# Attention's first two value projections: chunks taken in turn, and four sums in two wide PSUM tiles

## The chip, the cores and the metric

The kernel runs on one core of one Trainium2 chip. The metric is device time in microseconds (us) of one execution; lower is better. Times are medians of several runs. The profile is one execution more, taken by the hardware profiler; its span goes from the first to the last instruction.

## What is computed

The program is a decoder trunk of two layers on 256 tokens of width 1024 in float32. Each layer is a token mixer (stick-breaking attention beside MoBA attention, two branch projections, two sigmoid gates, one output projection) and a SwiGLU block, each followed by a residual and a layer norm. What matters here is the start of the mixer of the first layer:

```python
proj = x @ w_in
q_sb, k_sb, v_sb, q_mb, k_mb, v_mb, g_sb, g_mb = jnp.split(proj, cuts, axis=-1)
o_sb = stick_breaking_attention(heads(q_sb, 8), heads(k_sb, 8), heads(v_sb, 8))
o_mb = moba_attention(partial_rope(heads(q_mb, 8), pos), partial_rope(heads(k_mb, 8), pos), heads(v_mb, 8))
```

The first two outputs that the kernel makes are v_sb and v_mb, each 256 tokens by 512 columns.

## The kernel before, in words

**Products.** A float32 product is made of three passes of the rounded type float32r: both operands are split into a high part (a cast, `hi`) and a low part (the operand less its high part, `lo`), and TensorE adds hi·hi, hi·lo and lo·hi into one sum (`mm3`, whose matmuls all stand on L529). The cast runs on ScalarE (all on line L60, the helper `act`), the subtraction on VectorE (all on L65, the helper `dve`).

**Weights.** They come in chunks ("granules") of 128 x 1024 float32, 512 KB each, called by SyncE's queue into one of six `raw` buffers, and their two parts go into two rings `whi` and `wlo` of ten chunks each. A few chunks are split by DMA instead. The stream of chunks runs ahead of TensorE. A chunk's number is its place in the stream; the buffers are named after it, so `raw13` is chunk 13. The first four are loaded and split in two halves.

**What sets the order.** Each engine runs its instructions in the order in which they are written. The class `Weave` keeps an estimated clock while the program is written and decides by it where a chunk's split, or an eviction of a sum, is put among the instructions of ScalarE and VectorE. The very first splits stand in a table, `START`, with a time each.

**The start.** Twenty passes of zeros (`busy`, ten float32 matmuls of two recorded passes each) run on TensorE while the first data are on their way. `both_tokens` then makes v_sb (sums `l0pv0` and `l0pv1`, one for each half of the tokens, chunks 0 to 3) and after it v_mb (`l0pu0`, `l0pu1`, chunks 4 to 7). Chunk 0 is not split: `whole` multiplies it as float32 with the unsplit x (L564). The sums of v_sb lie in two PSUM tiles of one bank (the pool of `bankM`), those of v_mb in the first bank of two tiles of two banks (`banksB`). When a sum is done, `put` evicts it in two steps, a cast on ScalarE and a subtraction on VectorE, into `l0vsb` or `l0vmb`. Behind these stand the queries and keys (`l0pq`, `l0pk`, ...). Where an instruction writes a tile that another engine has read, the framework makes it wait on that engine's semaphore.

x itself comes transposed, in three pieces for each half of the tokens (`x00`, `x01`, `x02` for the first, `x10`, `x11`, `x12` for the second); ScalarE's queue loads the first four pieces, SyncE's the last two between the first chunks.

Of the kernel before, what the change touches and what calls it, by code (L numbers as in the profile page):

```python
# [10 lines left out]
AF = mybir.ActivationFunctionType  # L11
# [4 lines left out]
P = 128  # L16
# [5 lines left out]
WIDTH = 512  # L22
# [13 lines left out]
          ([("n", d)] if isinstance(d, int) else [("b", d[1]), ("a", d[0]), ("t", d[0]), ("u", d[0])])]  # L36
         for down in DOWN]
BASE = [sum(NG_LAYER - NFC + len(x) for x in STEPS[:l]) for l in range(DEPTH + 1)]
EARLY = [*range(4), *range(16, 20), 8, 14, 9, 15, *range(4, 8), 20, 24, 21, 25, *range(10, 14), 22, 23,
         *range(26, 40)]  # L40
NACT = 12
# [5 lines left out]
class Weave:  # L47
# [6 lines left out]
    def __init__(self):  # L54
        self.t = self.act_t = self.dve_t = self.pool_t = 0.0
        self.sides = []
        self.busy = False
# [51 lines left out]
class WeightStream:  # L109
# [2 lines left out]

    def __init__(self, nc, pool, w, total, weave, rings):
        self.nc, self.pool, self.w, self.total, self.weave = nc, pool, w, total, weave
        self.loaded, self.split = 0, NWHOLE
        self.done = -1
        self.free = {-1: 0.0}
        self.current = 0
        self.rings = rings
        self._lay()  # L120
        self.dma_t = 1.7
        self.raws, self.left = [], {0: 9.0}
        self.raw, self.parts, self.there, self.ready, self.dma = {}, {}, {}, {}, {}
# [61 lines left out]
    def put_aside(self, l, places):  # L185

        for g, parts in zip(filter(self.aside, range(BASE[l], BASE[l + 1])), places):
            self.parts[g] = parts
# [72 lines left out]
    def piece(self, g, i, e):  # L261

        if i == 0:
            self.parts[g] = tuple(ring[:, self.place[g]:self.place[g] + GCOLS] for ring in self.rings)
        (hi, lo), t, sl = self.parts[g], self.raw[g], self._pieces(g)[i]
        n = sl.stop - sl.start
        e = self.weave.act(e, n, self.nc.scalar.copy, hi[:, sl], t[:, sl])
        self.ready[g] = self.weave.dve(e, n, self.nc.vector.tensor_sub, lo[:, sl], t[:, sl], hi[:, sl].bitcast(F32))
        if sl.stop == GCOLS:
            self.raw.pop(g)  # L270
            self.left[g] = self.ready[g]
            self.split += 1
            self.load(g + 1 + NRAW)

# [6 lines left out]
    def take(self, g):  # L281
# [3 lines left out]
        while g in self.dma and g not in self.ready:  # L285
# [6 lines left out]
RING = 10 * GCOLS + LINES  # L292
NRAW = 6
NWHOLE = 1
START = (("x00", 4.4), ("x10", 5.4), ("x01", 6.4), ("w10", 6.4), ("w11", 7.4), ("x11", 7.4), ("w20", 8.2), ("x02", 9.0),
         ("w21", 9.7), ("x12", 10.3), ("w30", 11.0), ("w31", 11.7))
BY_DMA = ((18, 24, 28, 33, 38), (18, 24, 28, 33, 38))
ASIDE = ((), ())
X_AFTER = {(2, 0): (0, 2), (2, 1): (1, 2)}
NSPLIT = 10  # L300
HOLD = (8, 5)
FINE = 4
N_WARM = 10
LEAD = 2
LOAD = 1.46
DMA_HI = 6.0
# [12 lines left out]
def place(g):  # L319

    l, r = where(g)
    if r >= NG_LAYER - NFC:
        r = NG_LAYER - NFC + STEPS[l][r - (NG_LAYER - NFC)][1]
    return l * NG_LAYER + (EARLY[r] if r < len(EARLY) else r)


def where(g):

    l = sum(g >= b for b in BASE[1:-1])
    return l, g - BASE[l]  # L330

# [30 lines left out]
def hybrid_trunk_kernel(ctx: ExitStack, tc: tile.TileContext, w, xT_in, x_in, ln_in,  # L362
                        ident_in, mask_in, rope_in, out):
    nc = tc.nc
# [27 lines left out]
    def bankM(name, shape):  # L392
        ps = psM.tile(shape, F32, tag="M", name=name)
        m_last.append(bank_of(ps))
        if len(m_last) > 2:
            m_before[m_last[-1]] = m_last[-3]
            begin(ps)
        return ps
# [3 lines left out]
    def begin(ps):  # L402
        pe_after(m_free.get(m_before.get(bank_of(ps)), 0.0))

    def bank_of(ps):
        return getattr(ps, "tensor", ps).name
# [7 lines left out]
    def bankC(name, shape):  # L414
        held.append(weave.t)
        return psC.tile(shape, F32, tag="C", name=name)
# [31 lines left out]
    def banksB(name):  # L448
        return psB.tile([P, 2, 512], F32, tag="B", name=name)
# [12 lines left out]
    zero, mhalf = few[:, 0:1], few[:, 1:2]  # L462
# [6 lines left out]
    weave = Weave()  # L469
    ws = WeightStream(nc, wpool, w, BASE[-1], weave, (whi, wlo))  # L470
    act, dve, pool = weave.act, weave.dve, weave.pool
# [7 lines left out]
    warm = small.tile([P, 1], F32, tag="nmu", name="warm")  # L479
# [5 lines left out]
    busy = bankC("busy", [P, P])  # L485
    for i in range(N_WARM):
        nc.tensor.matmul(busy, zero.to_broadcast([P, P]), zero.to_broadcast([P, P]), start=True, stop=True)

    def load_xT(t, ks, queue):
        queue.dma_start(xT_raw[t][:, ks, :], xT_in[:, t, ks, :])  # L490
# [6 lines left out]

    kcs = [slice(0, 2), slice(2, 4), slice(4, 8)]
    ws.side = weave.add(ws.line(), last=True)
    for t, k in ((0, 0), (1, 0), (0, 1), (1, 1)):  # L500
        load_xT(t, kcs[k], nc.scalar)
    nc.scalar.activation(warm, zero, AF.Sigmoid)

    def between(g, i):
        if (g, i) in X_AFTER:
            t, k = X_AFTER[g, i]
            load_xT(t, kcs[k], nc.sync)

    ws.load(4, between)
    for (kind, a, b), e in START:  # L510
        if kind == "x":
            split_xT(int(a), kcs[int(b)], e)
        else:
            ws.piece(int(a), int(b), e)
    weave.t = 4.5

    def late_loads():
        nc.sync.dma_start(ident, ident_in)
# [16 lines left out]
    def mm3(o, s_hi, s_lo, m_hi, m_lo, start, stop, tick=True):  # L535
        mm(o, s_hi, m_hi, start, False)
        mm(o, s_hi, m_lo, False, False)
        mm(o, s_lo, m_hi, False, stop)
        if tick:
            weave.tick()  # L540
# [5 lines left out]
    def pe_after(e):  # L546
        weave.t = max(weave.t, e)
# [12 lines left out]
    def whole(o, g, t, first):  # L560

        raw = ws.raw[g].rearrange("p (k c) -> p k c", k=2)
        for k in range(2):
            nc.tensor.matmul(o, xT_raw[t][:, 2 * g + k, :], raw[:, k, :], start=first and k == 0, stop=False)  # L564
            weave.t += 4 * WIDTH / 2400.0
            weave.tick()

    def tok_major(o, g, t, first, last, k0):

        if g < NWHOLE:  # L570
            return whole(o, g, t, first)
        hi, lo = ws.take(g)
        hi = hi.rearrange("p (k c) -> p k c", k=2)
        lo = lo.rearrange("p (k c) -> p k c", k=2)
        for k in range(2):
            ts = slice(t * P, (t + 1) * P)
            mm3(o, xT_hi[:, k0 + k, ts], xT_lo[:, k0 + k, ts], hi[:, k, :], lo[:, k, :],
                first and k == 0, last and k == 1)

    def both_tokens(name, g0, put):  # L580

        acc = [banksB(f"{name}{t}")[:, 0, :] if g0 == 4 else bankM(f"{name}{t}", [P, WIDTH]) for t in range(2)]
        order = ((0, 0), (1, 0), (0, 1), (1, 1), (0, 2), (1, 2), (0, 3)) if g0 <= 4 else \
            ((0, 0), (0, 1), (0, 2), (1, 0), (1, 1), (0, 3), (1, 2))
        for t, k in order + ((1, 3),):
            tok_major(acc[t], g0 + k, t, k == 0, k == 3, 2 * k)
            if t == 1:
                ws.used(g0 + k)
            if k == 3:
                put(t, acc[t])  # L590

    def feat_major(o, g):

# [346 lines left out]
    for l in range(DEPTH):  # L940
        G = BASE[l]
        L = f"l{l}"
# [8 lines left out]
            split_v(v_mb[t], ps)  # L951

        if l == 0:
            both_tokens(f"{L}pv", G, put_v)
            both_tokens(f"{L}pu", G + 4, put_u)
        else:
            for t in range(2):
                weave.finish(norms[:t + 1])
                pe_after(xT_ready[t])
                for j, put in enumerate((put_v, put_u)):  # L960
                    ps = bankM(f"{L}pvu{j}{t}", [P, WIDTH])
                    for i in range(4):
                        g = G + 4 * j + i
                        tok_major(ps, g, t, i == 0, i == 3, 2 * i)
                        if t == 1:
                            ws.used(g)
                    put(t, ps)
# [64 lines left out]
        for d in range(2):  # L1032
            q, k = [qk["q", d][:, n] for n in range(2)], qk["k", d]
# [69 lines left out]
        for t in range(2):  # L1103
            acc = banksB(f"{L}pw{t}")
# [78 lines left out]
        for t in range(2):  # L1183
            weave.finish(norms[:t + 1])
            pe_after(xT_ready[t])
            for j in range(2):
                ps = bankM(f"{L}pft{t}{j}", [P, 512])
                for i in range(4):
                    g = G + 56 + 4 * j + i
                    tok_major(ps, g, t, i == 0, i == 3, 2 * i)  # L1190
                    if t == 1:
                        ws.used(g)
                sides.append(weave.start(h_line(f"{L}sg{t}{j}", ps, j, t)))
# [11 lines left out]
        acc = [banksB(f"{L}pd{t}") for t in range(2)]  # L1205
# [71 lines left out]
        g = G + NG_LAYER - NFC  # L1277
        late_half = []
        for n, d in enumerate(DOWN[l][:-HOLD[l]]):
# [16 lines left out]
            i = pairs.index(d)  # L1296
# [109 lines left out]
```

## Time and profile before

| | |
|---|---|
| median of 3 runs | 716.48 us (716.02 to 716.57) |
| the profiled execution | 716.68 us, its span 714.9 us |
| TensorE (PE) busy in the span | 706.7 us (99%) |
| weight loads (PEld), VectorE, ScalarE, GpSimd busy | 657.7, 599.5, 436.6, 35.0 us |
| HBM read | 139.69 MB, 197 GB/s over the span |
| first product of v_sb starts | 5.05 us |
| first product of the queries starts | 27.97 us |

PE is the matmul engine, PEld its weight loads, DVE VectorE, ACT ScalarE, SP SyncE, POOL GpSimd. A busy time is that of instructions on the engine; TensorE's matmuls overlap, so that its speed is read from the distance of their starts. In a timeline row stand the start, how long the row lasts (one instruction or several alike), the engine, the line, the operation, the tiles written and read, the count, and in brackets the idle time before it with what ended it. The rows of the changed kernel have the same names, with line numbers four or five higher.

### The profile page before, as it was taken

How to read it: one execution, taken by the hardware profiler on the slowest of the kernel's cores; microseconds unless marked ns; L12 is line 12 of the kernel's file. 1: busy time of each engine (PE TensorE's matmuls, PEld its weight loads, DVE VectorE, ACT ScalarE, POOL GpSimd, SP SyncE). 2: the span in 40 equal slices, each digit the busy share in tenths (PEclk: the TensorE clock that was granted, in tenths of full speed). 3: DMA queues.
4: the chain of work that ended last, by engine and by line, in shares of the span. 5: the costliest groups of instructions: out<-in, count | busy, mean ns of one | idle time of the engine just before them, and what ended most of it. 6: DMA issues, size and time to landing. Idle time of an engine off the chain costs nothing. (4 is left out here: it accounts for less than half of the span.)

```text
span 714.9 us, 13082 instructions
## 1 busy us (share of the span) xinstructions
PE 706.7 (99%) x5135; PEld 657.7 (92%) x5135; DVE 599.5 (84%) x920; ACT 436.6 (61%) x677; POOL 35.0 (5%) x61
## 2 busy tenths in 40 slices
PE   9999999999999999999999999999999999999995
PEld 7999999998899999988889999999888999999885
DVE  5989989797888777799887899987879878778987
ACT  5868977664565554456456787876456555544551
POOL 0200100000000000000000010000010000000002
PEclk9999999999999999999999999999999999999998
DMA  8977755565585664449559566745646856524451
GB/s 319 396 230 254 198 153 173 167 217 186 171 301 197 194 194 145 122 142 329 198 183 315 155 186 170 213 142 177 237 147 216 273 189 198 191 96 137 147 206 59
DMA packets 40526, 141.58 MB, mean 198 GB/s; under 512 B 4625, under 2 KB 5393, under 8 KB 40465
## 3 DMA queue, kind: packets, MB, share of 16 engines
q1 hardware_dynamic: 37008, 129.74, 53.1%
q0 software_dynamic: 2880, 10.49, 6.9%
q8 instruction: 40, 0.66, 0.4%
q10 hardware_dynamic: 576, 0.52, 0.2%
q14 instruction: 22, 0.17, 0.1%
HBM read 139.69 MB, written 1.05 MB: 197 GB/s over the span
## 5 line engine op out<-in xcount | busy, mean ns | idle before, releaser
L65 DVE TENSOR_TENSOR wlo<-raw,whi 128x1024 fp32r<-128x1024 f32 (+1 forms) x274 | 302.2, 1125 | 27.2 <-ACT whi L60 23.8
L60 ACT CAST whi<-raw 128x1024 fp32r<-128x1024 f32 (+1 forms) x274 | 260.2, 973 | 75.1 <-DVE raw L65 29.5
L529 PE MATMUL l0pf<-xT_hi,whi 128*128 128x256 f32 x288 | 79.6, 276 | 0.0
L529 PE MATMUL l1pf<-xT_hi,whi 128*128 128x256 f32 x288 | 79.6, 276 | 0.0
L529 PE MATMUL l0pf<-xT_lo,whi 128*128 128x256 f32 x288 | 79.5, 276 | 0.0
L529 PE MATMUL l0pf<-xT_hi,wlo 128*128 128x256 f32 x288 | 79.5, 276 | 0.0
L529 PE MATMUL l1pf<-xT_hi,wlo 128*128 128x256 f32 x288 | 79.5, 276 | 0.0
L529 PE MATMUL l1pf<-xT_lo,whi 128*128 128x256 f32 x288 | 79.5, 276 | 0.0
L529 PEld LDWEIGHTS l0pf<-xT_lo,whi 128*128 128x128 f32 x288 | 54.1, 188 | 0.0
L529 PEld LDWEIGHTS l1pf<-xT_lo,whi 128*128 128x128 f32 x288 | 54.1, 188 | 0.0
L529 PEld LDWEIGHTS l1pf<-xT_hi,whi 128*128 128x128 f32 x288 | 54.1, 188 | 0.0
L529 PEld LDWEIGHTS l0pf<-xT_hi,whi 128*128 128x128 f32 x288 | 54.1, 188 | 0.0
L529 PEld LDWEIGHTS l0pf<-xT_hi,wlo 128*128 128x128 f32 x288 | 54.1, 188 | 0.0
L529 PEld LDWEIGHTS l1pf<-xT_hi,wlo 128*128 128x128 f32 x288 | 54.1, 188 | 0.0
L529 PE MATMUL l0pg<-xT_hi,whi 128*128 128x256 f32 x128 | 35.8, 280 | 0.0
L529 PE MATMUL l1pg<-xT_hi,whi 128*128 128x256 f32 x128 | 35.8, 280 | 0.0
L529 PE MATMUL l0pg<-xT_hi,wlo 128*128 128x256 f32 x128 | 35.5, 277 | 0.0
L529 PE MATMUL l1pg<-xT_hi,wlo 128*128 128x256 f32 x128 | 35.5, 277 | 0.0
L529 PE MATMUL l1pg<-xT_lo,whi 128*128 128x256 f32 x128 | 35.5, 277 | 0.0
L529 PE MATMUL l0pg<-xT_lo,whi 128*128 128x256 f32 x128 | 35.5, 277 | 0.0
L65 DVE TENSOR_TENSOR l1sf<-l1sf,l1pf 128x256 f32<-128x256 f32 x36 | 15.1, 421 | 15.5 <-ACT l1sf L60 14.9
L60 ACT ACTIVATE l0sf<-l0pf 128x256 f32<-128x256 f32 x18 | 6.9, 385 | 31.2 <-PE l0pf L529 31.2
(485 smaller groups left out, 1941.0 us busy)
## 6 DMA issues: line engine op xcount, KB each, us to landing
raw<-in_w_dram SPq DMA_DIRECT2D x230, 512.0 KB, 4.2
whi<-in_w_dram POOLq DMA_DIRECT2D x10, 512.0 KB, 5.1
wlo<-in_w_dram POOLq DMA_DIRECT2D x10, 512.0 KB, 6.3
ln<-in_ln_dram SPq DMA_DIRECT2D x8, 512.0 KB, 5.9
raw<-in_w_dram SPq DMA_DIRECT2D x8, 256.0 KB, 4.6
x<-in_x_dram SPq DMA_DIRECT2D x2, 512.0 KB, 4.7
xT_raw<-in_xT_dram ACTq DMA_DIRECT2D x4, 128.0 KB, 4.8
xT_raw<-in_xT_dram SPq DMA_DIRECT2D x2, 256.0 KB, 5.1
```

Source lines behind the costliest of these rows:

```text
L60: f(*args, **kw)
L65: f(*args, **kw)
L529: nc.tensor.matmul(o, a, b, start=start, stop=stop)
```

## The change

1. **Chunks in turn.** The new list `FIRST` loads the chunks of v_sb and v_mb alternately (columns of `w_in` for v_sb on even places of the stream, for v_mb on odd ones), and `both_tokens` goes through both outputs together: for each of four steps, v_sb for both halves of the tokens, then v_mb for both.
2. **Four sums in two tiles.** There are now two tiles of two banks, one for each half of the tokens, named `l0pv0` and `l0pv1`. The first bank holds the sum of v_sb, the second that of v_mb. The tiles named `l0pu` are gone.
3. **Unsplit products for one half.** Chunk 0 is multiplied unsplit for the first half of the tokens only; for the second half it is split like all others, so that `START` has two entries more (`w00`, `w01`).
4. **Fourteen warming passes** (`N_WARM` 7) in place of twenty.
5. **Order of the first loads and splits.** ScalarE issues one load of x, then loads its activation table and runs its warming instruction, then issues the other three. `X_AFTER` puts the last two pieces of x one chunk later in SyncE's queue. `START` has other times and another order.

```diff
+FIRST = [0, 16, 1, 17, 2, 18, 3, 19]
...
-        self.loaded, self.split = 0, NWHOLE
+        self.loaded, self.split = 0, 0
...
         if sl.stop == GCOLS:
-            self.raw.pop(g)
-            self.left[g] = self.ready[g]
+            if g >= NWHOLE:
+                self.raw.pop(g)
+                self.left[g] = self.ready[g]
             self.split += 1
...
-START = (("x00", 4.4), ("x10", 5.4), ("x01", 6.4), ("w10", 6.4), ("w11", 7.4), ("x11", 7.4), ("w20", 8.2), ("x02", 9.0),
-         ("w21", 9.7), ("x12", 10.3), ("w30", 11.0), ("w31", 11.7))
+START = (("x00", 4.2), ("w00", 4.7), ("x10", 5.5), ("w01", 5.6), ("w10", 6.2), ("w11", 7.0), ("w20", 7.7), ("x01", 7.8),
+         ("w21", 8.3), ("x11", 8.5), ("w30", 9.4), ("w31", 10.4), ("x02", 10.6), ("x12", 11.2))
...
-X_AFTER = {(2, 0): (0, 2), (2, 1): (1, 2)}
+X_AFTER = {(3, 0): (0, 2), (3, 1): (1, 2)}
...
-N_WARM = 10
+N_WARM = 7
...
+    if l == 0 and r < len(FIRST):
+        return FIRST[r]
     return l * NG_LAYER + (EARLY[r] if r < len(EARLY) else r)
...
-    for t, k in ((0, 0), (1, 0), (0, 1), (1, 1)):
+    load_xT(0, kcs[0], nc.scalar)
+    nc.scalar.activation(warm, zero, AF.Sigmoid)
+    for t, k in ((1, 0), (0, 1), (1, 1)):
         load_xT(t, kcs[k], nc.scalar)
-    nc.scalar.activation(warm, zero, AF.Sigmoid)
...
-    weave.t = 4.5
+    weave.t = 5.1
...
-        if g < NWHOLE:
+        if g < NWHOLE and t == 0:
             return whole(o, g, t, first)
...
-    def both_tokens(name, g0, put):
-
-        acc = [banksB(f"{name}{t}")[:, 0, :] if g0 == 4 else bankM(f"{name}{t}", [P, WIDTH]) for t in range(2)]
-        order = ((0, 0), (1, 0), (0, 1), (1, 1), (0, 2), (1, 2), (0, 3)) if g0 <= 4 else \
-            ((0, 0), (0, 1), (0, 2), (1, 0), (1, 1), (0, 3), (1, 2))
-        for t, k in order + ((1, 3),):
-            tok_major(acc[t], g0 + k, t, k == 0, k == 3, 2 * k)
-            if t == 1:
-                ws.used(g0 + k)
-            if k == 3:
-                put(t, acc[t])
+    def both_tokens(names, g0, puts):
+
+        both = [banksB(f"{names[0]}{t}") for t in range(2)]
+        acc = [[two[:, n, :] for two in both] for n in range(2)]
+        for i in range(4):
+            for n in range(2):
+                for t in range(2):
+                    tok_major(acc[n][t], g0 + 2 * i + n, t, i == 0, i == 3, 2 * i)
+                    if i == 3:
+                        puts[n](t, acc[n][t])
+                ws.used(g0 + 2 * i + n)
...
-            both_tokens(f"{L}pv", G, put_v)
-            both_tokens(f"{L}pu", G + 4, put_u)
+            both_tokens((f"{L}pv", f"{L}pu"), G, (put_v, put_u))
```

From the first product of the queries on, the instructions of TensorE, GpSimd and SyncE stand in the same order as before, and those of ScalarE and VectorE from the split of chunk 16 on. Before that, the order of instructions differs at three places. In the rows below the digit after `l0pv` and `l0vsb` is the half of the tokens, the number after the underscore only tells tiles apart, and "waits" names the engine or the DMA queue whose semaphore the instruction waits for.

TensorE at the start, before:

```order
L487 MATMUL busy_103<-few_84 128x128 [waits DVE_49]
L487 MATMUL busy_103<-few_84 128x128 x9
L564 MATMUL l0pv0_173<-raw0_119,xT_raw0_92 128x512 [waits DMAHW1_49,DMAHW0_49]
L564 MATMUL l0pv0_173<-raw0_119,xT_raw0_92 128x512 [waits DMAHW3_49]
L564 MATMUL l0pv1_174<-raw0_119,xT_raw1_93 128x512 [waits DMAHW2_49]
L564 MATMUL l0pv1_174<-raw0_119,xT_raw1_93 128x512
L529 MATMUL l0pv0_173<-whi_89,xT_hi_85 128x512 [waits Activation_49]
```

and in the change:

```order
L491 MATMUL busy_103<-few_84 128x128 [waits DVE_49]
L491 MATMUL busy_103<-few_84 128x128 x6
L569 MATMUL l0pv0_174<-raw0_116,xT_raw0_92 128x512 [waits DMAHW1_49,DMAHW0_49]
L569 MATMUL l0pv0_174<-raw0_116,xT_raw0_92 128x512 [waits DMAHW2_49]
L534 MATMUL l0pv1_175<-whi_89,xT_hi_85 128x512 [waits Activation_49]
L534 MATMUL l0pv1_175<-wlo_91,xT_hi_85 128x512 [waits DVE_49]
L534 MATMUL l0pv1_175<-whi_89,xT_lo_86 128x512 [waits DVE_49]
L534 MATMUL l0pv1_175<-whi_89,xT_hi_85 128x512 [waits Activation_49]
```

Two of the four unsplit matmuls became six split ones, which wait for splits on both other engines.

TensorE at the last of the eight chunks (chunk 7), before:

```order
L529 MATMUL l0pu0_238<-whi_89,xT_hi_85 128x512 [waits Activation_49]
L529 MATMUL l0pu0_238<-wlo_91,xT_hi_85 128x512 [waits DVE_49]
L529 MATMUL l0pu0_238<-whi_89,xT_lo_86 128x512
L529 MATMUL l0pu0_238<-whi_89,xT_hi_85 128x512
L529 MATMUL l0pu0_238<-wlo_91,xT_hi_85 128x512
L529 MATMUL l0pu0_238<-whi_89,xT_lo_86 128x512
L529 MATMUL l0pu1_239<-whi_89,xT_hi_85 128x512
```

and in the change, up to the first product of the queries (without the rows that repeat these):

```order
L534 MATMUL l0pv0_174<-whi_89,xT_hi_85 128x512 [waits DVE_49]
L534 MATMUL l0pv0_174<-wlo_91,xT_hi_85 128x512
L534 MATMUL l0pv0_174<-whi_89,xT_lo_86 128x512
L534 MATMUL l0pv1_175<-whi_89,xT_hi_85 128x512 [waits DVE_49]
L534 MATMUL l0pv1_175<-wlo_91,xT_hi_85 128x512
L534 MATMUL l0pq0_329<-xT_hi_85,whi_89 128x256 [waits Activation_49]
```

The first matmul of each half now waits for VectorE, and the second one waits for nothing.

ScalarE and VectorE around the evictions of v_sb, before (ScalarE, then VectorE):

```order
L60 CAST whi_89<-raw7_149 128x1024 [waits DMAHW1_49]
L60 CAST l0vsb0_169<-l0pv0_173 128x8x64 [waits PE_49]
L60 CAST whi_89<-raw8_159 128x1024 [waits DMAHW2_49]
L60 CAST l0vsb1_170<-l0pv1_174 128x8x64 [waits PE_49]
L60 CAST whi_89<-raw9_167 128x1024 [waits DMAHW3_49]
```

```order
L65 TENSOR_TENSOR wlo_91<-raw7_149,whi_89 128x1024 [waits DMAHW1_49,Activation_49]
L65 TENSOR_TENSOR l0vsb0_169<-l0pv0_173,l0vsb0_169 128x8x64 [waits Activation_49]
L65 TENSOR_TENSOR l0vsb1_170<-l0pv1_174,l0vsb1_170 128x8x64 [waits Activation_49]
L65 TENSOR_TENSOR wlo_91<-raw8_159,whi_89 128x1024 [waits DMAHW2_49]
L65 TENSOR_TENSOR wlo_91<-raw9_167,whi_89 128x1024 [waits DMAHW3_49,Activation_49]
```

and in the change (ScalarE, then VectorE):

```order
L61 CAST whi_89<-raw12_227 128x16x32 [waits DVE_49,PE_49]
L61 CAST whi_89<-raw13_234 128x16x32 [waits DMAHW2_49,DVE_49,PE_49]
L61 CAST whi_89<-raw13_234 128x16x32 [waits DVE_49,PE_49]
L61 CAST l0vsb0_170<-l0pv0_174 128x8x64 [waits PE_49]
L61 CAST l0vsb1_171<-l0pv1_175 128x8x64 [waits PE_49]
L61 CAST whi_89<-raw14_244 128x16x32 [waits DMAHW3_49]
L61 CAST l0vmb0_172<-l0pv0_174 128x8x64 [waits DVE_49,PE_49]
```

```order
L66 TENSOR_TENSOR wlo_91<-raw12_227,whi_89 128x16x32 [waits Activation_49]
L66 TENSOR_TENSOR l0vsb0_170<-l0pv0_174,l0vsb0_170 128x8x64 [waits Activation_49]
L66 TENSOR_TENSOR wlo_91<-raw13_234,whi_89 128x16x32 [waits DMAHW2_49,DVE_49]
L66 TENSOR_TENSOR wlo_91<-raw13_234,whi_89 128x16x32 [waits DVE_49]
L66 TENSOR_TENSOR l0vsb1_171<-l0pv1_175,l0vsb1_171 128x8x64 [waits Activation_49]
```

The evictions of v_sb moved from behind chunk 7 to behind the casts of chunk 13 on ScalarE, and on VectorE to both sides of chunk 13.

## The prediction

> **What bounds the kernel now.** I read the busy times first, then the weight loads' waits, then the timeline of the first 32 us on each engine. From the page, and from the groups of waits (engine and line, what it waited for: us in total, times, longest):
>
> ```profile
> PE 706.7 (99%) x5135; PEld 657.7 (92%) x5135; DVE 599.5 (84%) x920; ACT 436.6 (61%) x677; POOL 35.0 (5%) x61
> PEld l0pv L529 <- DVE xT_lo L65: 0.4, 1, 0.4
> PEld l1sb_o L529 <- ACT whi L60: 0.2, 1, 0.2
> ```
>
> TensorE is the bound, and no wait of its weight loads that something else ended exceeds 0.4 us, but for the 0.9 us before the first pass. So whatever the start gains or loses should reach the end undiminished: the later order is unchanged, and there is no later stall in which a shift could disappear. The question is when the first product of the queries starts, now 27.97. TensorE's timeline until then (rows left out run at one speed):
>
> ```profile
> 0.91 4.30 PE L487 MATMUL busy<-few 128*128 128x128 f32 x20 [0.91 <-DVE few L484]
> 5.05 3.60 PE L564 MATMUL l0pv<-raw,xT_raw 128*128 128x512 f32 x8
> 8.72 0.40 PE L529 MATMUL l0pv<-wlo,xT_hi 128*128 128x512 f32 x1
> ...
> 12.36 0.39 PE L529 MATMUL l0pv<-whi,xT_lo 128*128 128x512 f32 x1
> 12.61 0.50 PE L529 MATMUL l0pv<-whi,xT_hi 128*128 128x512 f32 x1
> 12.95 0.40 PE L529 MATMUL l0pv<-wlo,xT_hi 128*128 128x512 f32 x1
> 13.33 0.50 PE L529 MATMUL l0pv<-whi,xT_lo 128*128 128x512 f32 x1
> 13.67 0.40 PE L529 MATMUL l0pv<-whi,xT_hi 128*128 128x512 f32 x1
> 13.90 0.39 PE L529 MATMUL l0pv<-wlo,xT_hi 128*128 128x512 f32 x1
> ...
> 27.74 0.39 PE L529 MATMUL l0pu<-whi,xT_lo 128*128 128x512 f32 x1
> 27.97 0.28 PE L529 MATMUL l0pq<-xT_hi,whi 128*128 128x256 f32 x1
> ```
>
> A split matmul of 512 columns takes 0.227 us from start to start (13.67 to 13.90), so six, one chunk for one half of the tokens, take 1.36 us. The four unsplit ones, recorded as eight, run from 5.05 to about 8.49 (0.23 before the row at 8.72): 0.86 us each. Between 12.36 and 13.67 four matmuls take 1.31 us in place of 0.91, a stall of 0.40 us.
>
> **The early terms.** Busy time of the warming passes in two stretches (PE, PEld, clock, DMA's share, GB/s):
>
> ```profile
> 1.50:4.50 3.00, 3.00 (x16) 3.00 (x16) 1.00 0.78 236
> 4.70:5.04 0.34, 0.34 (x4) 0.32 (x3) 1.00 0.83 253
> ```
>
> Sixteen passes, two of them in part, fill the first 3.0 us, 0.21 us each; four, one or two in part, the 0.34 us from 4.7 on, about 0.11 each. So fourteen end near 4.0 us, and whatever runs before about 4.7 us runs at half speed. The data for the first product are there at about 4.26, when ScalarE, free since 3.91 + 0.20 = 4.11, could begin its first cast:
>
> ```profile
> 3.91 0.20 ACT L502 ACTIVATE warm<-few 128x1 f32<-128x1 f32 x1
> 4.26 0.40 ACT L60 CAST xT_hi<-xT_raw 128x256 fp32r<-128x256 f32 x1
> 5.65 0.41 ACT L60 CAST xT_hi<-xT_raw 128x256 fp32r<-128x256 f32 x1 [0.99 <-DMA xT_raw<-in_xT_dram]
> 14.43 1.05 ACT L60 CAST whi<-raw 128x1024 fp32r<-128x1024 f32 x1 [0.63 <-DMA raw<-in_w_dram]
> 15.51 4.97 DVE L65 TENSOR_TENSOR wlo<-raw,whi 128x1024 fp32r<-128x1024 f32 x4 [0.98 <-ACT whi L60]
> ```
>
> So the products start 0.79 us earlier. Against that stand 0.22 us, half of the time from 4.26 to 4.7; waits of 0.1 us for the second half of chunk 0 and 0.3 us for splits of chunks 0 and 1 (the second half of x lands at 5.65, then cast and subtraction). Two unsplit matmuls less and six split ones more give 2 x 0.86 - 1.36 = 0.36 us. The old stall of 0.40 goes, since four products now share a piece of x. TensorE would reach chunk 4 at 4.26 + 0.22 + 1.72 + 0.4 + 7 x 1.36 = 16.1 us. Chunk 4 is cast from 14.43 on and its low part is ready at 15.51 + 1.22 = 16.7 (a quarter of four is 1.24): a wait of up to 0.4. With 2.72 us a chunk, TensorE has done chunks 4, 5 and 6 at 24.3 to 24.7 us, and with chunk 7 it would be through at 27.0 to 27.4. If this were all, the kernel would gain 0.6 to 0.95 us. The moved loads of x I cost at nothing: they queue behind the first piece's transfer, and the table load lies where ScalarE has nothing to cast. Without that cover each piece comes up to 1.5 us later (the table load and its warming instruction), which chunk 0 would pay in full; like all of these terms it would only shorten the stall below.
>
> **The new wait.** The order of the change shows what undoes this. In the first seven chunks the matmul with `whi` waits for ScalarE and the next, with `wlo`, for VectorE. At chunk 7 the first matmul of each half waits for VectorE, and the second waits for nothing. So the first one waits for something on VectorE that comes after chunk 7's low part. Chunk 7 goes into the v_mb half of `l0pv0`, and what VectorE does with that tile before is the eviction of v_sb from its other half. The semaphore count is that of this very subtraction, `l0vsb0` for the first half of the tokens and `l0vsb1` for the second. Before the change these sums lay in tiles of their own.
>
> On ScalarE the eviction of `l0vsb0` stands behind both casts of chunk 13. Those are paced by DMA:
>
> ```profile
> 22.68 1.05 ACT L60 CAST whi<-raw 128x1024 fp32r<-128x1024 f32 x1 [0.59 <-DMA raw<-in_w_dram]
> 24.30 1.05 ACT L60 CAST whi<-raw 128x1024 fp32r<-128x1024 f32 x1 [0.58 <-DMA raw<-in_w_dram]
> 25.53 1.14 ACT L60 CAST whi<-raw 128x512 fp32r<-128x512 f32 x2 [0.17 <-DMA raw<-in_w_dram]
> 26.75 1.15 ACT L60 CAST whi<-raw 128x512 fp32r<-128x512 f32 x2
> 26.53 3.69 DVE L65 TENSOR_TENSOR wlo<-raw,whi 128x512 fp32r<-128x512 f32 x6
> L60 ACT CAST l0vsb<-l0pv 128x512 fp32r<-128x512 f32 x2 | 1.2, 582 | 0.0
> L65 DVE TENSOR_TENSOR l0vsb<-l0pv,l0vsb 128x512 fp32r<-128x512 f32 x2 | 1.4, 687 | 0.1
> ```
>
> These are chunks 10 to 13, cast as they land; in the last two rows (groups: busy us, mean ns) are v_sb's evictions. The stretches of the DMA (last two columns its share and GB/s, the one before the granted clock) show that chunk 13 will not come much sooner:
>
> ```profile
> 9.50:12.50 3.00, 3.00 (x15) 2.35 (x13) 1.70 (x3) 1.24 (x3) 0.00 (x0) 1.00 0.92 294
> 12.50:30.00 17.50, 17.50 (x86) 14.45 (x85) 16.16 (x19) 14.68 (x21) 4.14 (x8) 1.00 1.02 404
> 707.70:711.20 3.50, 0.00 (x0) 0.00 (x0) 3.40 (x8) 0.00 (x0) 2.49 (x3) 1.00 0.39 150
> 711.30:714.90 3.60, 0.00 (x0) 0.00 (x0) 0.47 (x1) 0.00 (x0) 0.00 (x0) 0.50 0.38 146
> ```
>
> From 12.5 us on the queues are full at 404 GB/s, and the change moves the same bytes ahead of chunk 13. Only the dip at 9.5 to 12.5 us could be absent: 3.0 x (1 - 294/404) = 0.8 us sooner.
>
> So, step by step: ScalarE is done with chunk 13 at 26.75 + 1.15 = 27.9; `l0vsb0` is cast until 28.4, `l0vsb1` until 28.9 (0.5 each back to back); VectorE subtracts `l0vsb0` until 29.1 (0.69); TensorE starts chunk 7's first half at 29.1 to 29.2, after a stall of 4.4 to 4.9 us, and ends it at 30.5. VectorE takes both pieces of chunk 13 (3.69 / 6 = 0.61 each) until 30.3 and `l0vsb1` until 31.0; the second half starts there and ends at 32.35. A matmul that resumes after a wait takes 0.1 us more (12.61 to 12.95), so 32.4 to 32.5 us.
>
> **The sum.** 32.45 - 27.97 = +4.5 us. The early gains don't count in it: the end hangs on chunk 13's landing, and a faster start only lengthens the stall. Bounds: 0.8 us less without the dip, +3.7; to the other side, the clock. Queued behind the waiting matmul are all of TensorE's products; ScalarE and VectorE run on with the stream. What is late next is the eviction of v_mb and the queries, all by the same 4.5 us; the chunks gain slack by it. The profiled execution of 716.68 us would become 721.2; it lies 0.2 above the median of 716.48, so I forecast **721.0 us** beside the median.
>
> **Rivals.**
>
> *The clock falls in the stall.* TensorE has no matmul from 707.7 on (x0), and the granted clock is 1.00 until 711.2 and 0.50 from 711.3 on: it fell 3.5 us or a little more after the work stopped. The stall of 4.4 to 4.9 us is longer. If the clock falls before 29.1, the passes run at half speed until it is granted again; the first time this took from 0.91 to about 4.7, 3.8 us. Half of 2.9 to 3.8 us is 1.4 to 1.9 us, of which 0.5 lies in the wait for `l0vsb1` anyhow: +5.4 to +5.9 us, 721.9 to 722.4. Against it speaks that without the dip the stall is shorter by 0.8 us, and one such fall is all that the trace shows. The Trainium skill (TensorE: Matmul & The Clock Gate, Part 1) says that the clock falls after a window of about 3.4 us of idleness, and that the windows run freely; by that rule a stall of 4.5 us holds a whole window in about a third of the cases, and the time would be that of this rival then. The fall in this trace agrees with it.
>
> *The wait does not bind: the sums are free of each other.* Then only the early terms are left, -0.6 to -0.95 us: 715.5 to 715.9, not slower. It decides if the semaphore count of chunk 7's first matmul is reached by 24.7 us, thus if `l0vsb0` is evicted ahead of chunk 13. Against it stand the order of ScalarE and the DMA's pace; for it only that the counts could be less than I read. The Trainium skill (PSUM — Partial Sum Buffer, Terms) makes the bank, and not a wider tile, the thing that two engines must not touch at once. By that rule the products into one bank need no wait for the eviction of the other, and the time would be that of this rival; no run here shows such an overlap, and the order shows the wait.
>
> *A short stall.* If the stream lands 1.5 to 2.5 us sooner than the dip explains, as with a start at which DMA is fuller, +1.5 to +3 us: 718 to 719.5. The full queues speak against it.
>
> **Chances.** The stall without a fall of the clock 0.53 (719.9 to 721.5), with it 0.31 (to 723), the short stall 0.07, the wait that does not bind 0.06, anything above 723 us 0.03. The range from 719.5 to 722.9 us holds 8 in 10. About 0.2% (1.4 us) is what a measurement of this kernel can tell from no change: faster 0.02 (the early terms add up to at most 1.3 us even with no wait at all), the same 0.06, slower 0.92.
>
> **What would show it.** In the changed profile: first product at 4.2 to 4.3 us; chunk 7's first matmul at 28.3 to 29.2, with a gap of 3.5 to 5 us before it that VectorE's `l0vsb` ended; a second gap under 0.6 us at the other half; the first product of the queries at 31.6 to 32.5; and from there a constant shift to the end. A lower granted clock around 29 to 33 us would show the clock's rival. The forecast is wrong if no gap is there at chunk 7, or if it is there and the end of the kernel does not move with it.

## The result and the profile after

| | before | after |
|---|---|---|
| median | 716.88 us (716.02 to 717.75, 6 runs) | 722.49 us (720.56 to 723.41, 6 runs) |
| the profiled execution, its span | 716.68 us, 714.9 us | 722.26 us, 720.5 us |
| first product of v_sb | 5.05 us | 4.43 us |
| first product of the queries | 27.97 us | 33.50 us |

The ratio is 1.0074, with an interval from 1.0063 to 1.0084: slower by about 5.6 us. The prediction, 721.0 us in a range from 719.5 to 722.9, had the sign and the place right, and a size that was 1.5 us short. TensorE's timeline of the changed kernel shows both (`...` stands for rows left out):

```profile
4.43 2.88 PE L569 MATMUL l0pv<-raw,xT_raw 128*128 128x512 f32 x4 [0.17 <-DMA xT_raw<-in_xT_dram]
...
24.66 0.39 PE L534 MATMUL l0pv<-whi,xT_lo 128*128 128x512 f32 x1
28.98 0.50 PE L534 MATMUL l0pv<-whi,xT_hi 128*128 128x512 f32 x1 [3.93 <-DVE l0vsb L66]
...
30.02 0.50 PE L534 MATMUL l0pv<-wlo,xT_hi 128*128 128x512 f32 x1
30.32 0.63 PE L534 MATMUL l0pv<-whi,xT_lo 128*128 128x512 f32 x1
30.78 0.80 PE L534 MATMUL l0pv<-whi,xT_hi 128*128 128x512 f32 x1
...
32.65 0.63 PE L534 MATMUL l0pv<-wlo,xT_hi 128*128 128x512 f32 x1
33.08 0.63 PE L534 MATMUL l0pv<-whi,xT_lo 128*128 128x512 f32 x1
33.50 0.32 PE L534 MATMUL l0pq<-xT_hi,whi 128*128 128x256 f32 x1
```

Between 24.66 and 28.98 stands the predicted stall ahead of chunk 7, and the row names what ended it: VectorE's subtraction `l0vsb`. From 30.2 us on the matmuls start 0.43 us apart (32.65 to 33.08) instead of 0.227: half speed. The timelines of ScalarE (first fence) and VectorE (second), in the same trace, show the chain behind the stall:

```profile
22.65 1.05 ACT L61 CAST whi<-raw 128x1024 fp32r<-128x1024 f32 x1 [0.16 <-DMA raw<-in_w_dram]
25.35 2.36 ACT L61 CAST whi<-raw 128x512 fp32r<-128x512 f32 x4 [1.66 <-DMA raw<-in_w_dram]
27.62 1.06 ACT L61 CAST l0vsb<-l0pv 128x512 fp32r<-128x512 f32 x2
```

```profile
28.23 0.69 DVE L66 TENSOR_TENSOR l0vsb<-l0pv,l0vsb 128x512 fp32r<-128x512 f32 x1 [0.93 <-ACT l0vsb L61]
```

ScalarE sits idle 1.66 us until a chunk lands, casts chunks 12 and 13 (four halves), and only then evicts v_sb, whose last product had ended at 25.05 us (24.66 + 0.39). The clock is in the view by stretches (PE, PEld, VectorE, ScalarE and GpSimd busy, granted clock, DMA's share, GB/s):

```profile
24.96:28.98 4.02, 0.09 (x2) 0.01 (x1) 2.04 (x4) 3.54 (x7) 0.00 (x0) 1.00 1.03 421
28.98:30.17 1.19, 1.19 (x5) 1.00 (x6) 1.19 (x3) 0.75 (x2) 0.00 (x0) 1.00 1.01 413
30.18:33.58 3.40, 3.40 (x10) 2.27 (x9) 3.40 (x6) 1.62 (x3) 0.00 (x0) 0.50 0.65 220
33.60:36.00 2.40, 2.40 (x22) 2.40 (x21) 1.50 (x3) 2.26 (x3) 0.00 (x0) 1.00 0.79 256
```

The clock did not fall in the stall but 1.2 us after TensorE had resumed, and stayed at half for 3.41 us. After that the shift stays: +5.5 us at the queries, +5.6 in the span.

### The profile page after: what moved, and what is told of

It is laid out like the page before. It is cut to its first block, busy times and chain, and to the rows that moved or that the text cites. A ratio compares the mean times of both kernels' runs of the same rounds, so it can differ in the third digit from the quotient of the medians.

```text
span 720.5 us, 13080 instructions
## 1 busy us (share of the span) xinstructions
PE 708.3 (98%) x5131; PEld 658.6 (91%) x5131; DVE 601.2 (83%) x922; ACT 437.9 (61%) x679; POOL 33.5 (5%) x61
```

## The experiments

**The theory:** the two sums share one tile, so chunk 7's first product waits for the eviction of the other sum; that stands on ScalarE behind a chunk paced by DMA; the fall of the clock comes on top. **The rivals:** the loss sits in another part of the change (chunk order, unsplit products, warming, loads), or a shared tile costs something by itself, or the low clock is hidden by other waits.

**1. The evictions behind all products.** The wait has nothing to stand on.

```diff
-                    if i == 3:
-                        puts[n](t, acc[n][t])
+        for n in range(2):
+            for t in range(2):
+                puts[n](t, acc[n][t])
```

> The changed kernel, but the four sums are evicted after the products of all eight chunks instead of at each chunk's last product. Two wide tiles stay, the new chunk order too. No product then waits for an eviction that stands behind chunk 13. Theory (the wait of chunk 7's first product for the eviction of l0vsb is all of the loss): no stall before chunk 7; its two halves take 2 x 1.36 us after the last product of chunk 6 (24.66 + 0.23 in the profile of the change), so the queries start at 26.8 to 27.7 us, no fall of the clock near 30 us, and the time is 0.3 to 1.0 us below before: ratio 0.9985 to 0.9996. Rival (the loss is in what else the change does: the new chunk order, the smaller unsplit part, the fewer warming passes, the moved loads): the time stays 4 us or more above before, ratio 1.006 or more, with the queries after 31 us.

Measured: 716.46 us against 716.89, ratio 0.9994 (0.9985 to 1.0002). TensorE's timeline at the queries:

```profile
27.48 0.39 PE L534 MATMUL l0pv<-whi,xT_lo 128*128 128x512 f32 x1
27.71 0.28 PE L534 MATMUL l0pq<-xT_hi,whi 128*128 128x256 f32 x1
```

No wait for `l0vsb` is left in this trace, the clock does not fall before the end of the kernel, and the whole loss is gone, with the wide tiles, the chunk order and all the early parts in place.

**2. Four tiles of their own,** the evictions where the change has them.

```diff
-        both = [banksB(f"{names[0]}{t}") for t in range(2)]
-        acc = [[two[:, n, :] for two in both] for n in range(2)]
+        acc = [[bankC(f"{names[0]}{t}", [P, WIDTH]) for t in range(2)],
+               [banksB(f"{names[1]}{t}")[:, 0, :] for t in range(2)]]
```

> The changed kernel, but the four sums lie in four tiles of their own, as before the change, instead of pairwise in two wide tiles; the evictions stand where the change puts them, behind chunk 13 on ScalarE. Theory (the wait comes from the two sums having one tile): no wait for l0vsb at chunk 7, queries at 26.8 to 27.7 us, time 0.3 to 1.0 us below before, as with the late evictions. Rival (it is where the evictions stand that costs, the tile does not matter): a stall of 4 us or more stays before chunk 7, and the time is 721 to 723 us.

Measured: 716.58 us, ratio 0.9993 (0.9984 to 1.0002). From its timeline, rows of TensorE, ScalarE and VectorE:

```profile
27.55 0.28 PE L534 MATMUL l0pq<-xT_hi,whi 128*128 128x256 f32 x1
24.60 2.37 ACT L61 CAST whi<-raw 128x512 fp32r<-128x512 f32 x4 [0.90 <-DMA raw<-in_w_dram]
26.87 1.06 ACT L61 CAST l0vsb<-l0pv 128x512 fp32r<-128x512 f32 x2
27.48 0.69 DVE L66 TENSOR_TENSOR l0vsb<-l0pv,l0vsb 128x512 fp32r<-128x512 f32 x1 [0.93 <-ACT l0vsb L61]
```

The evictions still stand behind chunk 13 and come nearly as late as in the change (the subtraction at 27.48 instead of 28.23), and here it does not matter: TensorE begins the queries at 27.55 while v_sb is still being subtracted. So neither the late eviction (here) nor the shared tile (experiment 1) costs anything alone that these runs can tell. Both together do: the wait counts for a tile, and in the change the tile holds two sums.

**3. The shared tile alone, in the kernel before.**

```diff
+    shared = []
...
-        acc = [banksB(f"{name}{t}")[:, 0, :] if g0 == 4 else bankM(f"{name}{t}", [P, WIDTH]) for t in range(2)]
+        if g0 < 4:
+            shared.extend(banksB(f"{name}{t}") for t in range(2))
+        acc = [two[:, g0 // 4, :] for two in shared]
```

> The kernel before with one part of the change alone: v_sb and v_mb of one token half share a wide tile; chunk order, unsplit products, loads and warming as before. Chunk 4's first product for each half then waits until VectorE has subtracted l0vsb0 or l0vsb1. In the profile of before TensorE reaches chunk 4 at 17.1 us, and those subtractions end at 21.1 and 21.9 us. Theory (a shared tile makes the next sum's first product wait for the other sum's eviction): a gap of 3.5 to 4.3 us at about 17.1 us that VectorE's l0vsb ended, queries 3 to 4 us later if what follows cannot be caught up (the loads are slower than TensorE there, so up to half of the gap may be given back as later waits vanish: lower bound +1.5), up to +5.5 with a fall of the clock: 718.4 to 722.4 us. Rival (a shared tile costs nothing by itself): 716.5 to 717.2 us, no such gap.

Measured: 722.93 us, ratio 1.0077 (1.0061 to 1.0093): +6.0 us, 0.5 us above the upper end of what was expected. TensorE's timeline in this kernel, and then two stretches of it:

```profile
16.97 0.39 PE L529 MATMUL l0pv<-whi,xT_lo 128*128 128x512 f32 x1
21.25 0.50 PE L529 MATMUL l0pv<-whi,xT_hi 128*128 128x512 f32 x1 [3.89 <-DVE l0vsb L65]
...
33.91 0.28 PE L529 MATMUL l0pq<-xT_hi,whi 128*128 128x256 f32 x1
```

```profile
21.25:22.66 1.41, 1.41 (x6) 1.19 (x7) 1.38 (x2) 0.95 (x2) 1.37 (x6) 1.00 1.03 421
22.67:26.07 3.40, 3.40 (x10) 2.62 (x9) 3.40 (x4) 2.91 (x4) 2.77 (x3) 0.50 1.02 410
```

One part of the change, the shared tiles, put into the kernel before, makes the same stall at its own place, and the same fall of the clock after it. The gap is as expected (3.5 to 4.3 us). Nothing was caught up: the queries start 5.9 us later.

**4. The stall filled with work.** The wait stays, TensorE multiplies zeros meanwhile (no output uses them).

```diff
+                    if i == 3 and n == 1 and t == 0:
+                        for _ in range(N_FILL):
+                            nc.tensor.matmul(busy, zero.to_broadcast([P, P]), zero.to_broadcast([P, P]), start=True, stop=True)
```

> The changed kernel with eighteen additional float32 products of zeros into the warming tile (36 passes of about 0.11 us, 4.0 us) on TensorE directly ahead of chunk 7's first product, so that the stall is filled with work that no output uses. The wait itself stays. Theory (of the 5.6 us lost, about 4.3 are the wait and 1.3 the fall of the clock to half speed that follows it): granted clock 1.00 through 24 to 34 us, chunk 7 starts at 28.9 to 29.3 us, the queries at 32.1 to 32.5 instead of 33.5 us, the time about 721, 1.1 to 1.6 us below the change where the change's clock falls. Rival (the low clock after the stall is hidden by the second wait, for l0vsb1, and by the loads): queries at 33 us or later and a time of 722.3 to 722.8 us, as the change.

Measured: 720.82 us, ratio 1.0054 (1.0042 to 1.0067). TensorE's timeline, and then one stretch:

```profile
24.14 4.18 PE L595 MATMUL busy<-few 128*128 128x128 f32 x36
28.97 0.50 PE L535 MATMUL l0pv<-whi,xT_hi 128*128 128x512 f32 x1 [0.65 <-DVE l0vsb L66]
30.77 0.50 PE L535 MATMUL l0pv<-whi,xT_hi 128*128 128x512 f32 x1
...
32.26 0.28 PE L535 MATMUL l0pq<-xT_hi,whi 128*128 128x256 f32 x1
```

```profile
30.20:33.58 3.38, 3.23 (x20) 2.56 (x19) 3.38 (x6) 2.74 (x5) 0.00 (x0) 1.00 0.78 287
```

Chunk 7 starts at 28.97 as in the change (28.98), but the clock stays at 1.00, and the queries start at 32.26 instead of 33.50. So the wait is worth 32.26 - 27.97 = 4.3 us and the clock 1.24 us; by the ratios (1.0074 and 1.0054) the clock is 0.0020, or 1.4 us, though the two intervals just overlap. One of the five runs took 722.00 us with a mean clock of 0.998, so without a fall; what it lost was not seen in a trace.

**5. and 6. The evictions of v_sb one and two chunks further ahead on ScalarE.** One number is changed in the estimate by which the order is written, the assumed arrival time of the weight stream. It leaves the order on TensorE and GpSimd as it is:

```diff
-        self.dma_t = 1.7
+        self.dma_t = 3.2
```

(4.7 in the second.)

> The changed kernel, with the order book's arrival time of the weight stream set to 3.2 instead of 1.7, which moves one thing near the stall: on ScalarE the evictions of l0vsb stand ahead of the casts of chunk 13 instead of behind them. The shared tiles and the wait stay. Theory (the length of the stall is set by the cast of a chunk that DMA delivers): l0vsb0 is cast when chunk 12's casts end, about 1.2 us sooner (chunks land 1.2 us apart), so chunk 7 starts at 27.7 to 28.0 instead of 28.98 us, a stall of about 3 us; the time is 1.0 to 1.4 us below the change if the clock still falls (721.0 to 721.6), and 2.3 to 2.8 us below it if this shorter gap no longer makes it fall (719.6 to 720.3). Rival (the stall has another cause, and ScalarE's place of the eviction is only the sign of it): no change, 722.3 to 722.8 us.

> As the run before, with the arrival time 4.7, by which ScalarE evicts l0vsb ahead of chunk 12's casts already. In the change chunk 12 is cast from 25.35 us on, and the last product of v_sb ends at about 24.3 (first half) and 24.9 us (second). Theory: l0vsb0 is cast at 24.4 and subtracted by 25.6, so at chunk 7 a stall of 0.7 us or less is left, no fall of the clock, queries at 27.8 to 28.6 us, and the time is within 0.9 us of before (716.3 to 717.6), with the shared tiles in place. Rival (a shared tile costs several us wherever the evictions stand): above 719 us.

Measured, ahead of chunk 13: 719.98 us, ratio 1.0047 (1.0031 to 1.0062), four runs from 719.31 to 722.75. The longest is the profiled one (rows of TensorE and ScalarE from its timeline, then three stretches):

```profile
27.96 0.80 PE L534 MATMUL l0pv<-whi,xT_hi 128*128 128x512 f32 x1 [2.72 <-DVE l0vsb L66]
25.56 1.14 ACT L61 CAST whi<-raw 128x512 fp32r<-128x512 f32 x2 [1.69 <-DMA raw<-in_w_dram]
26.61 1.07 ACT L61 CAST l0vsb<-l0pv 128x512 fp32r<-128x512 f32 x2
```

```profile
24.96:27.32 2.36, 0.28 (x2) 0.00 (x0) 0.28 (x2) 1.76 (x4) 0.00 (x0) 1.00 1.02 418
27.33:27.96 0.63, 0.00 (x0) 0.00 (x1) 0.63 (x2) 0.63 (x2) 0.00 (x0) 0.50 1.04 423
27.96:34.14 6.18, 6.18 (x17) 5.02 (x18) 4.88 (x9) 3.02 (x7) 0.00 (x0) 0.50 0.75 256
```

The stall is shorter by a chunk's pace, as expected (2.72 us idle in place of 3.93). The expectation on the clock was wrong in this execution (721.0 to 721.6 us with a fall): it fell 2.1 us into the gap (25.24 to 27.33) and stayed low for 6.8 us, so that this run, at 722.75 us, took as long as the change itself. Two of the other three runs had a mean clock of 0.998 and took 719.3 and 719.7 us; the profiled one had 0.992.

Ahead of chunk 12: 718.14 us, ratio 1.0021 (1.0011 to 1.0032), 717.02 to 720.44. That is 0.5 us above what the theory gave (716.3 to 717.6). Two more traces of this kernel and one of the change show where a part of the spread comes from:

> A second trace of the kernel that evicts l0vsb ahead of chunk 12's casts, whose times lie between 717.0 and 720.4 us while its first trace has one of the shortest. Theory: the evictions still stand behind the cast of a chunk that DMA delivers, chunk 11; in the traces so far the one landing that comes about 2.5 us late falls on different chunks, and where it falls on chunk 10 or 11 the stall before chunk 7 grows from 0.5 to as much as 2.5 us. So a run of 718.5 us or more shows a gap of 1.5 us or more at chunk 7 that VectorE's l0vsb ended, with ScalarE waiting for DMA ahead of it, and a run under 718 us shows a gap under 1 us. Rival: the spread comes from somewhere else, and a long run shows no longer gap there.

> As the look before: the gap at chunk 7 by which the run's time can be told, 0.5 us in a run of 717 us, 2 us in one of 719 us; the rival expects no relation.

> A second trace of the changed kernel itself. Theory: its time is the stall plus, where the clock falls, 1.3 us: with the clock at 1.00 through 24 to 34 us the queries start at 31.9 to 32.4 us and the time is 720.5 to 721.2 us; with a fall the queries start at 33.0 to 34.0 us and the time is 721.9 to 723.4 us. Rival: the times between 720.6 and 723.4 us come from how soon chunk 13 lands, and the clock has no part in them.

The waits of the weight loads for `l0vsb` (us, times, longest), in the three traces of 717.20, 718.10 and 718.85 us, in this order:

```profile
PEld l0pv L534 <- DVE l0vsb L66: 1.0, 2, 0.5
```

```profile
PEld l0pv L534 <- DVE l0vsb L66: 1.3, 2, 0.8
PEld l0pd L534 <- DVE wlo L66: 0.7, 1, 0.7
```

```profile
PEld l0pv L534 <- DVE l0vsb L66: 2.1, 2, 1.6
```

ScalarE's timeline in the third:

```profile
24.33 1.05 ACT L61 CAST whi<-raw 128x1024 fp32r<-128x1024 f32 x1 [0.16 <-DMA raw<-in_w_dram]
25.28 1.07 ACT L61 CAST l0vsb<-l0pv 128x512 fp32r<-128x512 f32 x2
```

In these three traces the time follows the wait. In the third the wait follows the landing of chunk 11: it lands at 24.25 us and is cast at 24.33, and the evictions stand behind it; in the first it lands at 22.99, in the second at 23.16. The 718.10 us of the second hold half a microsecond that comes much later, in the SwiGLU block (`l0pd`, 0.7 us where the other two have 0.2). A gap of 2 us was expected in a run of 719 us; it was 1.2 us, so the direction is shown and the expected size was too large. What the run of 720.44 us lost was not seen in a trace; its mean clock of 0.994, where the other eight have 0.997 or more, speaks for a fall.

The second trace of the change, at 722.58 us, shows the fall again, at 30.08 us with the queries at 33.16, as the theory's case with a fall says. Two stretches of it:

```profile
28.64:30.07 1.43, 1.43 (x6) 1.04 (x6) 1.43 (x3) 0.75 (x2) 0.00 (x0) 1.00 1.02 418
30.09:33.48 3.39, 3.31 (x9) 2.46 (x9) 3.30 (x6) 1.70 (x4) 0.00 (x0) 0.50 0.82 274
```

No trace shows a run of the change without a fall; that of 720.56 us, with a mean clock of 0.998, is most likely one.

**7. and 8. Two early parts undone, with four tiles of their own.** All twenty warming passes (`N_WARM` 10); and chunk 0 unsplit for both halves:

```diff
-        if g < NWHOLE and t == 0:
+        if g < NWHOLE:
...
-START = (("x00", 4.2), ("w00", 4.7), ("x10", 5.5), ("w01", 5.6), ...
+START = (("x00", 4.2), ("x10", 5.5), ...
```

> The kernel with four tiles of their own (the stall gone), with all twenty warming passes in place of fourteen. It prices the smaller warming alone. By the sum of the prediction the warming passes then hold TensorE until about 5.05 to 5.3 us instead of 4.4 to 4.6, of which half a microsecond reaches the queries (later waits for splits and landings take the rest): queries at 27.9 to 28.2 us against 27.55, time 0.2 to 0.6 us above that of the four tiles, ratio to before 0.9990 to 1.0010. Rival (the fewer passes cost as much as they save, since the clock rises later): the same time as with four tiles or 0.1 to 0.4 us less.

> The kernel with four tiles of their own (the stall gone), with chunk 0 unsplit for both token halves again (eight recorded float32 products, no split of chunk 0 on ScalarE and VectorE). It prices this part alone. By the prediction's sum two float32 products at 0.86 us replace six split ones of 0.227: TensorE 0.36 us longer, less the waits for the splits of chunk 0 and x (0.1 to 0.3): queries 0.1 to 0.4 us later than with four tiles (27.65 to 27.95 us), time 0 to 0.4 us above it. Rival (the split of chunk 0 delays the other casts more than it saves): queries earlier than 27.5 us, time below it.

Measured: 716.69 us with twenty passes, ratio 0.9993 (0.9984 to 1.0001), and 716.77 us with both halves unsplit, 0.9994 (0.9986 to 1.0003), beside 0.9993 without either. So no gain from either part can be told from nothing. The traces missed their expectations in opposite directions: the queries start at 27.34 us with more warming passes (27.9 to 28.2 expected) and at 28.25 us with both halves unsplit (27.65 to 27.95 expected). What differs is when the clock was first granted, by the trace's clock record: 4.98 us in the one and 7.02 in the other, 6.01 with the four tiles. At half speed a microsecond more costs half a one, so corrected to 6.01 they would be 27.85 and 27.75 by this estimate; it is argued, not shown. And with twenty passes the start at 27.34 was lost again at the first scores:

```profile
41.63 1.44 PE L534 MATMUL l0sb_s<-l0sb0k,l0sbq 64*128 64x256 f32 x20 [0.63 <-DVE l0sb0k L66]
```

## Why the prediction was right, and where its size was off

- **The new wait.** Right in place and cause, and close in length: chunk 7 at 28.98 us (28.3 to 29.2 named as the evidence, 29.1 to 29.2 in the sum), ended by `l0vsb`, and a second wait of 0.5 us at the other half (under 0.6). Experiments 1 and 2 each take one of its two conditions away, and the wait is gone; 3 makes it in the kernel before by the shared tile alone, since the evictions there already stood behind the casts of chunks 7 and 8.
- **What paces it.** Right: the cast of a chunk that DMA delivers. Moving the evictions ahead of one chunk took 1.2 us of idle time away, ahead of two nearly all of it, and what was left varied with the landing of the next chunk up. That the length came out so near is in part luck, as two stretches of the changed kernel show:

```profile
9.50:12.50 3.00, 3.00 (x15) 2.49 (x14) 2.17 (x5) 1.91 (x5) 0.00 (x0) 1.00 1.00 359
22.57:25.25 2.68, 2.48 (x11) 1.70 (x10) 2.39 (x2) 1.05 (x1) 0.00 (x0) 1.00 1.01 408
```

The dip that the prediction took as a bound was in good part gone (359 GB/s instead of 294), and chunk 11 was cast at 22.65 instead of 24.30 us: 1.65 us sooner, twice the 0.8 us that was allowed for. Then chunk 12 landed at 25.25 us, 2.68 us after chunk 11 (22.57) instead of the usual 1.2, with the queues full all the while, and chunk 13 came at 26.48 us against 26.67 before. Without this gap the wait would have cost about 2.8 us instead of 4.3, an estimate from these landings, and that is in the range of the rival "a short stall" (0.07). One such gap of 1.6 to 2.7 us between two landings stands in 12 of the 13 traces between 20 and 29 us, on chunks that vary; its cause is not shown.

- **The clock: the term that was mis-sized.** The sum gave this zero and the rival 0.31. Its size, 1.24 us in the trace, agrees with the rival's 0.9 to 1.4 (+5.4 to +5.9 less 4.5), and the queries at 33.50 are 5.5 us late, inside it. Its chance was set too low. A fall of 3.41 us takes 0.0024 off the mean clock. The kernels without a stall have 0.996 to 0.999; of the six runs of the change three have 0.992 to 0.995, which speaks for a fall, two have 0.996, which leaves it open, and the one with 0.998 is the fastest (720.56 us), 0.4 below the forecast. Both profiled executions of the change fell. The step that failed is the reading that the clock falls only after 3.5 us or more without any work, taken from the one fall at the end of the kernel before. The Trainium skill (TensorE: Matmul & The Clock Gate, Part 1) has the clock fall after an idle window of about 3.4 us; by that rule the odds were a third, an estimate from the page's figure. In both traces of the change the fall ends a window in which TensorE had worked for 1.2 and 1.4 us of 3.41, so that rule of the Trainium skill and the traces differ, and the measurement decides. That the windows run freely, as the same part of the Trainium skill says, is borne out: between two changes of the clock in one trace lies a multiple of 3.413 us each time.
- **The early terms.** The prediction had them at -0.6 to -0.95 us if no wait bound. With the wait gone (1 and 2) the queries start 0.26 and 0.42 us earlier than before and the time is 0.4 us less, with an interval from -1.1 to +0.1. So the gain was set too high, though the interval does not exclude it. Two steps can be behind that. The first clock was taken to come at 4.7 us, as in the one trace of before; it came at 6.6 and 6.0 in these two. And "there is no later stall in which a shift could disappear" held for a loss, not for a gain: in experiment 7 a start 0.63 us earlier met a wait of 0.63 us at the first scores. What each of the two took from the gain is not shown.
- **The other side.** "The wait does not bind" (0.06) is what experiments 1 and 2 made true; it gave 715.5 to 715.9 us, and they take 716.46 and 716.58. The rule set beside it, that the bank is what two engines must not share at once (the Trainium skill, PSUM — Partial Sum Buffer, Terms), did not save the change, since the wait in it goes by the tile; no run here let an eviction and a product overlap in two banks of one tile.

No kernel here beats the one before by more than the runs can tell: the four without the wait each have a ratio of 0.9993 or 0.9994, with intervals that reach above 1. Whether chunk order, loads or warming bring the 0.4 us stays open.

## What to carry to other kernels

When sums are packed into one tile, look at what waits for the tile as a whole: in this kernel the next product into one sum waited for the eviction of the other, where that eviction was written ahead of it, and the price was set by whatever the eviction was queued behind. The packing or the late eviction alone cost nothing here that could be told, so either can be kept if the other is given up. A long stall on TensorE can be dearer than its length: in all four traces with 2.7 to 3.9 us of idle time the clock fell for it, for 3.4 or 6.8 us, and in the change that put 1.24 us on top; after the 1.2 us of experiment 6 it did not fall.

## What the runs showed of the hardware

- **The clock can fall after the work has resumed.** In each trace its changes lie whole multiples of 3.413 us apart, which gives windows of that length. Those that ended in a fall held 1.2 us of TensorE's busy time (35%) in the change, 1.4 in its second trace (42%), 1.4 in experiment 3 (41%) and 1.3 in experiment 5 (39%); none was idle as a whole. The windows just before them, with 50, 49 and 45% in the first three, did not end in a fall, nor did one with 65% (the third trace of experiment 6, from 23.54 to 26.96 us; two stretches of it):

```profile
25.45:26.64 1.19, 0.00 (x0) 0.00 (x1) 0.75 (x2) 1.19 (x3) 0.00 (x0) 1.00 1.02 417
26.64:34.00 7.36, 7.28 (x48) 6.42 (x49) 7.36 (x12) 5.04 (x10) 0.75 (x1) 1.00 0.87 278
```

The windows in which the work of a kernel ends agree: in seven traces they held 8 to 44% (44 in experiment 8) and ended in a fall, in six they held 47 to 93% (47 in experiment 2) and did not. In these traces, then, the line lies between 44 and 45% of a window.

- **It came back only after a fuller window.** In experiment 5 the window from 27.33 to 30.74 us was busy from 27.96 on, 81% of it, and the next was still at half speed; in the change one window, full, was enough. The same holds at the start: in all 13 traces the first grant ended a window with 90% or more, and the window ahead of that one held at most 79%.
- **The first grant is not set by the kernel alone.** In the 13 traces it came between 4.18 and 7.02 us; in three whose starts are written alike (the change, its second trace, experiment 4) at 6.28, 6.19 and 4.18 us. The work up to it runs at half speed: a warming pass took 0.21 us before the grant and 0.11 after it in the kernel before, though the view shows 1.00 there, since the clock record begins with the first grant. So this alone can move the start by an estimated 1.4 us (half of 2.84) between traces, more than the early parts of the change could bring.
